# The gate modulation of layer 0 and all of layer 1's modulation from transposed weights, summed along the row

## The chip, the cores and the metric

The kernel runs on one core of a Trainium2 chip. The metric is the device time of one execution in microseconds (us), given as the median of several runs. The engines named below are PE (TensorE, the matmuls), PEld (TensorE's weight loads, which overlap its matmuls), DVE (VectorE), ACT (ScalarE), POOL (GpSimd) and SP (SyncE, which here issues nearly all transfers). Each engine runs its own list of instructions strictly in order; an instruction whose input is not ready holds everything behind it on that engine.

## The reference

Two layers work on 1024 latent and 256 context tokens of width 1024. Each layer first scales and shifts the normed tokens with numbers that come from a conditioning vector, and at its end multiplies the branch's output by a gate from the same source:

```python
def modulation(cond, w, b):                      # cond (1024,), w (1024, 3072)
    m = jax.nn.silu(cond) @ w + b
    return jnp.split(m, 3, axis=-1)              # shift, scale, gate
...
for i in range(DEPTH):                           # two layers
    sh_l, sc_l, g_l = modulation(c, mod_w[i], mod_b[i])
    sh_c, sc_c, g_c = modulation(c_ctx, mod_w[i], mod_b[i])
    h_lat = rms_norm(x_lat, norm_g[i]) * (1.0 + sc_l[:, None, :]) + sh_l[:, None, :]
    h_ctx = rms_norm(x_ctx, norm_g[i]) * (1.0 + sc_c) + sh_c
    ...                                          # even: two attentions; odd: convolution, neighbourhood attention
    x_lat = x_lat + g_l[:, None, :] * y_lat
    if update_ctx:                               # layer 0 only
        x_ctx = x_ctx + g_c * y_ctx
return rms_norm(x_lat, final_g)
```

The modulation is thus a product of a 1024 x 3072 matrix with two vectors ("conditions" 0 and 1), per layer. Layer 0 needs shift and scale (parts 0 and 1) before anything else, its gate (part 2) only after the attention. Layer 1 needs shift and scale when layer 0 is done, and its gate for condition 0 alone.

## The kernel before

All large matmuls are done as three products of a high and a low half (`mm3`, L320 to L322), so every operand is split: ACT casts the high half and POOL or DVE subtracts it (`split`, L298 and L301).

The program has these stages (times from the trace). To about 80 us, the first loads, layer 0's shift and scale, the norm and the inputs `h`. To about 160 us, the projections of the first of four attention units (`fill0(0)`, the flag `solo` being set). To about 640 us, attention units 2, 3, 0 and 1 in that order, each woven by `weave` with the projections of the next. From about 640 to 900 us, the last unit's attention, woven with layer 0's output projection (`out0_part`, weights `wr` from `ev_wo`). Then layer 1.

A scheduler writes each engine's list from priorities. `later(LATE)` puts work behind other work that is ready (`LATE` is 100), and `issue_after` makes an instruction wait for another one, its anchor, on the anchor's engine.

The modulation is computed in two ways. `mod_half` (L171 to L191) uses PE with the weights as the moving operand, in the first stage only. `mod_half_v` (L195 to L234) makes 512 columns of one part for one or two conditions. It loads blocks of 128 rows of `mod_w` (two together, 512 KB, while `solo`; else one, 256 KB), and DVE adds each, times the condition's value of that row, into an accumulator `macc` of 128 x 512 (L216 for the first, L221 for the others; outside `solo` a few go to ACT and POOL by the table `MODP`, L218 and L219). Then PE sums each accumulator over the partitions with four matmuls against a vector of ones (`trm`, L227; each shows as two in the trace's counts), and DVE adds the bias (L228). The result `modT[l]` holds 24 columns per condition, column `o` being outputs 128 o to 128 o + 127.

Of layer 0's shift and scale one half-part goes through `mod_half_v` (the event "v" of `PLAN`) and three through `mod_half` ("m"). Layer 0's gate and all of layer 1 (seven steps of two conditions, and the gate of layer 1 for one) are made by the generator `mod_steps`. `tick`, called at every third row block of a projection, advances it: at each call while `solo` (`TICK0` 1), at every third call later (`TICK1` 3). The last of its sums starts at 439.6 us.

The other names in this text: `QL` (L390) is the low half of queries, DVE's work, which PE's scores `st` wait for; `mp` (L580, L591) is the maximum over a row of scores `mx`, `nmt` (L379) what is made of it; `qs` (L301) is the split of projected queries and keys; `x` at L1012 is the residual plus gate times the output projection `po`; `Od`, `gt`, `QH` and `QL` on SP are transfers of the attention's operands and results; `pl`, `gl` and `wl` are low halves of weights or probabilities made by a subtraction on POOL or DVE.

Of the kernel before, what the change touches and what calls it, by code (L numbers as in the profile page):

```python
# [18 lines left out]
P = 128  # L19
# [32 lines left out]
MWB, WRB = 2, 2  # L52
# [21 lines left out]
TICK0, TICK1 = (1, 3)  # L74
# [15 lines left out]
def tile_kernel(ctx: ExitStack, tc: tile.TileContext, a, out):  # L90
# [11 lines left out]
    mk, mwp, hold, layer = [0], [None], [0], [0]  # L102
# [10 lines left out]
    def nm(s):  # L113
        uid[0] += 1
        return f"{s}_{uid[0]}"
# [79 lines left out]
    def mod_half_v(pool, l, part, j, conds):  # L195

        c0 = part * 1024 + j * 512
        pool, tag, bufs = (kvp, "QH", 3) if mwp[0] is not None else (pool, "macc", 2)
        accs = [pool.tile([P, 512], F32, tag=tag, name=nm("macc"), bufs=bufs) for _ in conds]
        pre = []  # L200
        for dk in range(DK):
            if solo[0] and dk % 2 == 0:
                w2 = mw_tile()
                d_ = SY.dma_start(w2, a["mod_w"][l, dk * P : (dk + 2) * P, c0 : c0 + 512].rearrange("(d p) n -> p d n", d=2))
                if mwp[0] is not None:
                    mm0.append(d_)
                pre = [w2[:, 0, :], w2[:, 1, :]]
            if pre:
                w = pre.pop(0)
                hold[0] = len(pre)  # L210
            else:
                w = pool.tile([P, 512], F32, tag="mw", name=nm("mw"), bufs=MWB)
                SY.dma_start(w, a["mod_w"][l, dk * P : (dk + 1) * P, c0 : c0 + 512])
            for q, t in zip(conds, accs):
                if dk == 0:
                    VE.tensor_scalar(t, w, csil[:, dk, q : q + 1], None, op0=ALU.mult)  # L216
                elif dk in MODP[q] and not solo[0]:
                    SC.activation(w, w, AF.Identity, scale=csil[:, dk, q : q + 1])  # L218
                    GP.tensor_tensor(t, t, w, op=ALU.add)  # L219
                else:  # L220
                    VE.scalar_tensor_tensor(t, w, csil[:, dk, q : q + 1], t, op0=ALU.mult, op1=ALU.add)  # L221
            yield
        o = part * 8 + j * 4
        for n_, (q, t) in enumerate(zip(conds, accs)):
            tr = bank("ov" if solo[0] else "tr", nm("trm"))
# [8 lines left out]
        yield  # L234
# [419 lines left out]
    with ExitStack() as p0x:  # L654
# [6 lines left out]
        with tc.tile_pool(name="st0", bufs=1, reuse_waits="tile") as st0:  # L661
# [38 lines left out]
            for ev in PLAN:  # L700
# [13 lines left out]
                elif ev == "v":  # L714
                    run(mod_half_v(st0, 0, *mh.pop(0), (0, 1)))
# [25 lines left out]
        def tick():  # L741
            beat[0] += 1
            if beat[0] % (TICK0 if solo[0] else TICK1) == 0:
                with later(LATE):
                    if mark[0] is None or solo[0]:
                        next(mods, None)
                    else:
                        with tc.issue_after(mark[0].ins):
                            next(mods, None)
# [128 lines left out]
        while hold[0]:  # L878
            next(mods)
# [96 lines left out]
    with tc.tile_pool(name="o0", bufs=1, reuse_waits="tile", side="right") as op_:  # L976
# [3 lines left out]
        x1 = []  # L980
        def load_oh(fs):
# [33 lines left out]
        def out0_part(fs):  # L1015
            for e2 in range(4):
# [58 lines left out]
        weave(main, NSTEP[U1 // 2] - GL - O1[0] - O1[1] - O1[2], through_attention(), O1[3])  # L1075
        a0x.close()
# [506 lines left out]
def _layout(i):  # L1583
    i = {n: np.asarray(i[n]) for n in _INS}

    def pk(v):
        return v.reshape(-1, P).T
# [5 lines left out]
    d["mod_w"] = i["mod_w"]  # L1593
# [49 lines left out]
```

## Time and profile before

| quantity | value |
|---|---|
| median of 3 runs | 1566.65 us (1564.84 to 1571.33) |
| span of the profiled execution | 1569.6 us |
| modulation weights loaded by SP | 34 transfers of 512 KB and 28 of 256 KB |
| the accumulations of L221 and L216 on DVE | 123, from 14.3 to 439.6 us |
| the sums of L227 on PE | 128 counted, from 33.5 to 442.0 us |

The profiled execution has no time beside its span; the span is the figure that stands next to the runs' times, 2.95 us above their median. In the profile a line of instructions reads: line, engine, operation, output from inputs with partitions x elements, the count, then busy time and the mean in ns of one, then the idle time ahead of them with what ended it. In a timeline a row reads start, duration, engine, line, operation, and in brackets the idle time ahead of it with what released it. A window row gives, for each engine, busy microseconds and the number of instructions in brackets, then the clock granted to PE as a share of full speed (PEclk), the share of time the transfer engines were busy, and the bytes moved.

### The profile page before, as it was taken

The page shows a single profiled execution, that of the slowest core. Times are in us where ns is not written, and L with a number is a line of the kernel's source. Part 1 is how long each engine was busy: PE and PEld are TensorE (multiplying, and loading weights), DVE is VectorE, ACT ScalarE, POOL GpSimd, SP SyncE. Part 2 cuts the span into 40 slices and gives each one's busy share as a digit, 9 for nine tenths or more (in the row PEclk, how much of TensorE's full clock was granted, in tenths as well). Part 3 has the DMA queues.
Part 4 walks back from the last instruction along what each step waited for, and adds up shares of the span by engine and source line. Part 5 has one row for each costly group of instructions (what it writes and reads, how often), then busy time and mean ns, then how long its engine had stood idle before and what let it go on. Part 6 is the DMA issues. An engine that isn't in the chain of part 4 may idle for free.

```text
span 1569.6 us, 22251 instructions
## 1 busy us (share of the span) xinstructions
PE 1460.8 (93%) x6984; PEld 1178.9 (75%) x6984; DVE 1129.4 (72%) x2172; ACT 762.0 (49%) x1545; POOL 830.0 (53%) x762
## 2 busy tenths in 40 slices
PE   6989999998999999899999889999999999899995
PEld 1878877876888677588887568888887787677784
DVE  4898896797768677455488668999654466776776
ACT  2721354545454754655555746443343445545472
POOL 1561463555465675756545756665443333444575
PEclk9899999999999999999999989999999999799897
DMA  9548245424431225612112022214547888889632
GB/s 337 190 142 260 87 142 167 132 67 125 154 116 47 67 91 167 224 47 61 48 38 85 14 94 61 81 58 148 177 154 224 237 229 242 248 231 251 187 95 108
DMA packets 199438, 221.03 MB, mean 141 GB/s; under 512 B 18956, under 2 KB 155352, under 8 KB 199320
## 3 DMA queue, kind: packets, MB, share of 16 engines
q1 hardware_dynamic: 192656, 208.04, 43.5%
q10 hardware_dynamic: 6664, 11.57, 2.3%
q8 instruction: 55, 0.90, 0.2%
q14 instruction: 63, 0.52, 0.1%
HBM read 159.51 MB, written 60.03 MB: 140 GB/s over the span
## 4 chain that ended last, share of the span: by engine, by line
PE 65%; DVE 14%; DMA 11%; issue 4%; POOL 2%; SPq 2%; ACT 1%; ACTq 0%; DVEq 0%; POOLq 0%
PE p L322 6%; PE p L321 6%; PE p L320 6%; PE ov L411 4%; PE ov L413 4%; PE ov L412 4%; PE po L320 4%; PE po L321 4%; PE po L322 4%; PE st L467 4%; PE st L471 4%; DMA mw<-in_mod_w_dram 3%; DVE macc L221 2%; PE pq L322 2%; PE pq L321 2%
## 5 line engine op out<-in xcount | busy, mean ns | idle before, releaser
L301 POOL TENSOR_TENSOR pl<-pf,ph 128x512 fp32r<-128x512 f32 (+4 forms) x321 | 393.7, 1237 | 320.1 <-ACT ph L298 260.0
L301 POOL TENSOR_TENSOR wl<-wr,wh 128x256 fp32r<-128x256 f32 (+2 forms) x256 | 197.5, 788 | 203.1 <-ACT wh L298 192.4
L479 ACT ACTIVATE pf<-st 128x512 f32<-128x512 f32 x284 | 167.3, 597 | 177.4 <-PE st L471 138.3
L298 ACT CAST ph<-pf 128x512 fp32r<-128x512 f32 (+4 forms) x364 | 210.5, 588 | 28.9 <-PE ov L412 21.5
L298 ACT CAST wh<-wr 128x256 fp32r<-128x256 f32 (+2 forms) x264 | 102.8, 404 | 172.9 <-DMA wr<-in_ev_qkv_dram 40.4
L320 PE MATMUL p<-hh,wh 128*128 128x512 f32 x448 | 177.5, 398 | 2.9 <-DVE spk L301 1.5
L321 PE MATMUL p<-hl,wh 128*128 128x512 f32 x448 | 178.0, 398 | 0.2 <-POOL hl L301 0.2
L322 PE MATMUL p<-hh,wl 128*128 128x512 f32 x448 | 175.9, 400 | 0.1
L467 PE MATMUL st<-QH,KAt 128*128 128x512 f32 (+4 forms) x364 | 145.4, 401 | 11.4 <-ACT pf L479 9.7
L411 PE MATMUL ov<-ph,Vt 128*128 128x512 f32 (+4 forms) x364 | 143.5, 394 | 9.7 <-ACT ph L298 5.0
L413 PE MATMUL ov<-pl,Vt 128*128 128x512 f32 (+4 forms) x364 | 144.1, 396 | 6.8 <-POOL pl L301 3.6
L471 PE MATMUL st<-QL,KBt 68*128 68x512 f32 (+4 forms) x364 | 139.0, 391 | 5.8 <-DVE QL L390 5.7
L412 PE MATMUL ov<-ph,Vt 128*64 128x512 f32 (+4 forms) x364 | 140.5, 386 | 0.0
L1122 DVE SCALAR_TENSOR_TENSOR cps<-U,taps,cps 128x512 f32<-128x512 f32 x184 | 124.3, 748 | 0.0
L591 DVE TENSOR_REDUCE mp<-mx 128x1 f32<-128x512 f32 x128 | 85.7, 682 | 42.5 <-PE mx L590 41.8
L221 DVE SCALAR_TENSOR_TENSOR macc<-mw,csil,macc 128x512 f32<-128x512 f32 x107 | 94.5, 901 | 17.5 <-DMA mw<-in_mod_w_dram 16.7
L320 PEld LDWEIGHTS p<-hh,wh 128*128 128x128 f32 x448 | 84.6, 189 | 23.6 <-DVE spk L301 1.7
L321 PEld LDWEIGHTS p<-hl,wh 128*128 128x128 f32 x448 | 84.5, 189 | 20.4 <-POOL hl L301 0.6
L322 PEld LDWEIGHTS p<-hh,wl 128*128 128x128 f32 x448 | 84.8, 189 | 20.1 <-POOL wl L301 0.6
L467 PEld LDWEIGHTS st<-QH,KAt 128*128 128x128 f32 x364 | 71.2, 196 | 33.4 <-ACT pf L479 17.6
L413 PEld LDWEIGHTS ov<-pl,Vt 128*128 128x128 f32 x364 | 71.1, 195 | 32.5 <-POOL pl L301 7.8
L411 PEld LDWEIGHTS ov<-ph,Vt 128*128 128x128 f32 x364 | 71.3, 196 | 27.3 <-ACT ph L298 8.4
(277 smaller groups left out, 3546.2 us busy)
## 6 DMA issues: line engine op xcount, KB each, us to landing
mw<-in_mod_w_dram SPq DMA_DIRECT2D x34, 512.0 KB, 5.9
Q<-qs SPq DMA_DIRECT2D x40, 256.0 KB, 2.7
QH<-Q SPq DMA_DIRECT2D x80, 128.0 KB, 2.8
wr<-in_od_d_dram SPq DMA_DIRECT2D x64, 128.0 KB, 2.7
mw<-in_mod_w_dram SPq DMA_DIRECT2D x28, 256.0 KB, 3.3
wr<-in_ev_qkv_dram SPq DMA_DIRECT2D x32, 192.0 KB, 3.6
KAt<-KD SPq DMA_DIRECT2D x16, 384.0 KB, 6.2
wr<-in_od_wo_dram SPq DMA_DIRECT2D x48, 128.0 KB, 3.2
```

Of the source, the lines that this page charges most:

```text
L221: VE.scalar_tensor_tensor(t, w, csil[:, dk, q : q + 1], t, op0=ALU.mult, op1=ALU.add)
L298: SC.copy(hi, src)
L301: (GP if leng == "g" else VE).tensor_tensor(lo, src, hi.bitcast(F32), op=ALU.subtract)
L320: PE.matmul(o, lh, rh, start=first, stop=False)
L321: PE.matmul(o, lh, rl, start=False, stop=False)
L322: done[0] = PE.matmul(o, ll, rh, start=False, stop=last)
L411: PE.matmul(o, V[:, 64:192], ph[:, :n], start=(t == 0), stop=False)
L412: PE.matmul(g.ov[0:64, q0 : q0 + n], V[:, 0:64], ph[:, :n], start=False, stop=False)
L413: pvs.append(PE.matmul(o, V[:, 64:192], pl[:, :n], start=False, stop=(last and g.sink is None)))
L467: sts.append(PE.matmul(st[:, :n], KA[:, cs], g.QH[:, q0 : q0 + n], start=True, stop=False))
L471: PE.matmul(st[:, :n], KB[0:68, cs], g.QL[0:68, q0 : q0 + n], start=False, stop=True)
L479: SC.activation(pf[:, :n], st[:, :n], AF.Exp, scale=1.0 if g.bias else SCALE)
```

## The change

`mod_half_v` is kept for the event "v" alone. Everything that `mod_steps` made is now made by `mod_rows` from `mod_wt`, a copy of the weights that the host gives transposed: one row is one output. A unit loads 128 rows of 1024 (512 KB, L241), and one DVE instruction (L251) multiplies them by `cb`, the condition's silu values laid out along the row and copied to all 128 partitions, sums along the row, and starts from the bias; the sum is one column of `modT`. In the order listing it shows as two rows, the product in place and the reading of the sum. There are 16 units for layer 0's gate (8 per condition), 24 for layer 1 condition 0 and 16 for condition 1: 56 in all. `cond_rows` makes the silu'd conditions as rows in DRAM (`csd`); `cb` is loaded from there four times in all, once for each condition of each layer.

The places and the buffers differ too. Layer 0's units use one buffer, and are advanced at every third beat, but no longer while `solo`. Layer 1's units use two buffers that an earlier stage has left free (`KB` and `KA` of the pool `a0`), and are advanced once after each block of layer 0's output projection, in the last attention unit. The anchor of `issue_after` is now `sts[-MLAG]`, a matmul of the scores.

The loads of modulation weights come to about 8.4 MB as blocks of `mod_w` and 56 x 0.524 = 29.4 MB as rows of `mod_wt`, against 34 x 0.524 + 28 x 0.262 = 25.2 MB before.

```diff
-MWB, WRB = 2, 2
+WRB = 2
-TICK0, TICK1 = (1, 3)
+TICK = 3
+MLAG = 2
...
-    def mod_half_v(pool, l, part, j, conds):
+    def mod_half_v(l, part, j, conds):
...
+    csd = dram("csd", [2, 1024])
+
+    def cond_rows(c_, t_):
+        SY.dma_start(c_[0:2, :], a["crow"])
+        SC.activation(t_[0:2, :], c_[0:2, :], AF.Tanh, scale=0.5)
+        VE.scalar_tensor_tensor(c_[0:2, :], t_[0:2, :], 1.0, c_[0:2, :], op0=ALU.add, op1=ALU.mult)
+        SY.dma_start(csd, c_[0:2, :])
+
+    def mod_rows(l, q, parts, cb, wt):
+        SY.dma_start(cb, csd[q : q + 1, :].broadcast_to([P, 1024]))
+        todo = [part * 8 + b for part in parts for b in range(8)]
+        ws = {}
+
+        def load(k):
+            o = todo[k]
+            ws[k] = wt()
+            r0 = (o - 16 if l == 0 else 8 + o) * P
+            SY.dma_start(ws[k], a["mod_wt"][r0 : r0 + P, :])
+
+        for k, o in enumerate(todo):
+            if l == 0:
+                load(k)
+                yield
+            else:
+                for k2 in range(k and k + 1, min(k + 2, len(todo))):
+                    load(k2)
+            w = ws.pop(k)
+            VE.tensor_tensor_reduce(out=w, in0=w, in1=cb, op0=ALU.mult, op1=ALU.add, scale=0.5,
+                                    scalar=modb[:, l, o : o + 1], accum_out=modT[l][:, o, q : q + 1])
+            if o == 15:
+                VE.scalar_tensor_tensor(gs[l][:, :, q], modT[l][:, 8:16, q], 1.0, normg[:, l, :], op0=ALU.add, op1=ALU.mult)
+            yield
...
         def tick():
             beat[0] += 1
-            if beat[0] % (TICK0 if solo[0] else TICK1) == 0:
-                with later(LATE):
-                    if mark[0] is None or solo[0]:
-                        next(mods, None)
-                    else:
-                        with tc.issue_after(mark[0].ins):
-                            next(mods, None)
+            if not solo[0] and beat[0] % TICK == 0:
+                with later(LATE), tc.issue_after(sts[-MLAG].ins if len(sts) >= MLAG else mark[0].ins):
+                    next(mods, None)
...
         def mod_steps():
-            for part in (2,):
-                for j in range(2):
-                    yield from mod_half_v(ap, 0, part, j, (0, 1))
-            for part in range(3):
-                for j in range(2):
-                    yield from mod_half_v(ap, 1, part, j, (0, 1) if part < 2 else (0,))
+            cb = ap.tile([P, 1024], F32, tag="cb", name="cb0")
+            wt = lambda: ap.tile([P, 1024], F32, tag="mw", name=nm("mw"))
+            cond_rows(cb, wt())
+            for q in range(2):
+                yield from mod_rows(0, q, (2,), cb, wt)
...
+        spare = [a0.tile([P, NTOK], F32, tag=t, name=nm("mw1"), bufs=2)[:, 0:1024] for t in ("KB", "KA")]
+        cb1 = a0.tile([P, 1920], F32, tag="V", name="cb1", bufs=2)[:, 0:1024]
+
+        def wt1():
+            spare.append(spare.pop(0))
+            return spare[-1]
+
+        mods1 = chain(mod_rows(1, 0, (1, 0, 2), cb1, wt1), mod_rows(1, 1, (1, 0), cb1, wt1))
...
                     for c in range(3):
                         yield from out0(fs, e, c, *w)
+                        with later(LATE), tc.issue_after(sts[-MLAG].ins):
+                            next(mods1, None)
...
         weave(main, NSTEP[U1 // 2] - GL - O1[0] - O1[1] - O1[2], through_attention(), O1[3])
+        run(mods1)
```

The first place is DVE in the first unit's projections, about 95 us into the run before. `macc` and `mw` are accumulators and weights of the modulation, `rt` and `pc` belong to the rotary step. Before:

```order
L830 TENSOR_TENSOR pc_750<-pc_750,k_cs 128x2x320
L221 SCALAR_TENSOR_TENSOR macc_588<-mw_637,csil,macc_588 128x512
L221 SCALAR_TENSOR_TENSOR macc_589<-mw_637,csil,macc_589 128x512
L301 TENSOR_TENSOR qs_842<-trk_838,qs_842 128x384
L221 SCALAR_TENSOR_TENSOR macc_588<-mw_637,csil,macc_588 128x512
```

In the same place now:

```order
L322 TENSOR_TENSOR qs_732<-trk_728,qs_732 128x384
L845 TENSOR_TENSOR rt_123_772<-pc_701,k_cs 128x320 x2
L847 TENSOR_TENSOR pc_701<-pc_701,k_cs 128x2x320
L322 TENSOR_TENSOR qs_767<-trk_763,qs_767 128x384
L845 TENSOR_TENSOR rt_132_852<-pc_781,k_cs 128x320 x2
L847 TENSOR_TENSOR pc_781<-pc_781,k_cs 128x2x320
```

The accumulations between the splits `qs` and the rotary steps are gone; nothing of the modulation stands there.

The second place is DVE while the second unit is projected (135 to 227 us before), where layer 0's gate is now made. `modT_90` is layer 0's result. Before, accumulations for both layers stood here:

```order
L221 SCALAR_TENSOR_TENSOR macc_1018<-mw_1108,csil,macc_1018 128x512 x2
L221 SCALAR_TENSOR_TENSOR macc_1018<-mw_1152,csil,macc_1018 128x512
L228 TENSOR_TENSOR modT_91<-trm_1176,modb 128x4
L221 SCALAR_TENSOR_TENSOR macc_1018<-mw_1152,csil,macc_1018 128x512
L216 TENSOR_SCALAR macc_1217<-mw_1219,csil 128x512
```

Now:

```order
L251 ISA mw_1560,modT_90<-mw_1560,cb_1139,modb 128x1024
L251 ISA modT_90 128x1
L406 TENSOR_TENSOR nmt_1332<-se_1334,nmt_1332 128x4
L601 TENSOR_REDUCE mp_1438<-mx_1440 128x2
L601 TENSOR_REDUCE mp_1438<-mx_1457 128x2
L251 ISA mw_1723,modT_90<-mw_1723,cb_1139,modb 128x1024
L251 ISA modT_90 128x1
L411 TENSOR_TENSOR QL_1117<-trn_1349,k_bd 12x512
```

Sums stand one by one ahead of `nmt`, `mp` and `QL`, each on the same buffer, whose next load follows the sum. The 16 sums of layer 0 stand within some 135 rows of DVE.

The third place is the last attention unit, on DVE and on SP, where layer 1 is now made. `mp` is the attention's, `x` the output projection's. DVE before, from about 790 us:

```order
L591 TENSOR_REDUCE mp_8269<-mx_8317 128x1
L1012 SCALAR_TENSOR_TENSOR x_1892_7482<-po_8764,modT_90,x_1892_7482 128x512
L591 TENSOR_REDUCE mp_8269<-mx_8320 128x1
L423 RECIPROCAL r_2126_8348<-r_2125_8347 128x8
L1012 SCALAR_TENSOR_TENSOR x_1901_7508<-po_8790,modT_90,x_1901_7508 128x512
```

DVE now:

```order
L251 ISA mw_1820_7188,modT_91<-mw_1820_7188,cb_7190,modb 128x1024
L251 ISA modT_91 128x1
L612 TENSOR_REDUCE mp_8055<-mx_8148 128x1
L612 TENSOR_REDUCE mp_8055<-mx_8151 128x1
L444 RECIPROCAL r_2071_8136<-r_2070_8135 128x8
L251 ISA mw_1821_7189,modT_91<-mw_1821_7189,cb_7190,modb 128x1024
L251 ISA modT_91 128x1
L1035 SCALAR_TENSOR_TENSOR x_1837_7231<-po_8719,modT_90,x_1837_7231 128x512
```

The sums stand between the same instructions as before. Layer 1's 40 sums (80 rows) stand within 200 rows of DVE, and PE's list has 504 rows beside these. On SP there, before:

```order
L331 DMA wr_8732<-in_ev_wo_dram 128x256
L331 DMA wr_8738<-in_ev_wo_dram 128x256
L331 DMA wr_8857<-in_ev_wo_dram 128x256
L331 DMA wr_8863<-in_ev_wo_dram 128x256
L565 DMA QH_7861<-Q_5_114 64x2x256 x2
L565 DMA QL_7862<-Q_5_114 64x2x256
```

SP now:

```order
L241 DMA mw_1820_7188<-in_mod_wt_dram 128x1024
L352 DMA wr_9052<-in_ev_wo_dram 128x256
L241 DMA mw_1821_7189<-in_mod_wt_dram 128x1024
L352 DMA wr_9058<-in_ev_wo_dram 128x256
L241 DMA mw_1820_7188<-in_mod_wt_dram 128x1024
L241 DMA mw_1821_7189<-in_mod_wt_dram 128x1024
L241 DMA mw_1820_7188<-in_mod_wt_dram 128x1024
L590 DMA gt_8242<-G_149 128x2x128
L241 DMA mw_1821_7189<-in_mod_wt_dram 128x1024
L352 DMA wr_9064<-in_ev_wo_dram 128x256
```

Each load of `mw` waits on SP until the sum before it on the same buffer is done, and what follows in SP's list (weights `wr`, gates `gt`) is issued after it.

More of the change, by code (lines that the diff above doesn't have):

```diff
@@ L101, in tile_kernel @@
     turn = [0, 0]
-    mk, mwp, hold, layer = [0], [None], [0], [0]
+    mk, mwp, layer = [0], [None], [0]
     sts, pvs = [], []
@@ L223, in mod_half_v @@
         o = part * 8 + j * 4
-        for n_, (q, t) in enumerate(zip(conds, accs)):
-            tr = bank("ov" if solo[0] else "tr", nm("trm"))
+        for q, t in zip(conds, accs):
+            tr = bank("ov", nm("trm"))
             for i in range(4):
@@ L1593, in _layout @@
     d["mod_w"] = i["mod_w"]
+    d["mod_wt"] = np.concatenate([i["mod_w"][0][:, 2048:].T, i["mod_w"][1].T])
+    d["crow"] = np.stack([i["c"][0], i["c_ctx"]])
     d["mod_b"] = np.stack([pk(i["mod_b"][l]) for l in range(2)], 1)
```

41 lines of the change are left out of this document (12 added, 29 removed).

## Prediction

> **What bounds the kernel now.** I read the page first (engines, the chain that ended last, the transfers), then a table of busy times by stretch, then the tiles of the modulation, then timelines at the places where PE waits.
>
> ```profile
> span 1569.6 us, 22251 instructions
> PE 1460.8 (93%) x6984; PEld 1178.9 (75%) x6984; DVE 1129.4 (72%) x2172; ACT 762.0 (49%) x1545; POOL 830.0 (53%) x762
> PE 65%; DVE 14%; DMA 11%; issue 4%; POOL 2%; SPq 2%; ACT 1%; ACTq 0%; DVEq 0%; POOLq 0%
> L221 DVE SCALAR_TENSOR_TENSOR macc<-mw,csil,macc 128x512 f32<-128x512 f32 x107 | 94.5, 901 | 17.5 <-DMA mw<-in_mod_w_dram 16.7
> mw<-in_mod_w_dram SPq DMA_DIRECT2D x34, 512.0 KB, 5.9
> mw<-in_mod_w_dram SPq DMA_DIRECT2D x28, 256.0 KB, 3.3
> ```
>
> PE is busy 93% of the span and holds 65% of the chain, so a microsecond taken from PE's own work counts nearly whole, and DVE time counts only where PE waits for it. Where that is, the table by stretch tells (busy microseconds, instructions in brackets):
>
> ```profile
> core 0: us, PE busy (x) PEld busy (x) DVE busy (x) ACT busy (x) POOL busy (x), PEclk, DMA share, GB/s
> 80.00:130.00 50.00, 42.27 (x245) 38.45 (x244) 47.31 (x61) 12.82 (x30) 28.16 (x19) 0.97 0.59 176
> 135.00:227.00 92.00, 87.79 (x472) 76.69 (x471) 81.35 (x160) 33.24 (x76) 39.71 (x33) 0.96 0.45 138
> 227.00:450.00 223.00, 209.80 (x1072) 174.95 (x1071) 175.50 (x388) 106.17 (x236) 114.47 (x97) 0.98 0.44 133
> 450.00:525.00 75.00, 73.97 (x364) 62.02 (x363) 53.67 (x99) 40.57 (x76) 48.07 (x38) 1.00 0.18 53
> 700.00:800.00 100.00, 100.00 (x482) 81.12 (x482) 59.39 (x111) 50.99 (x94) 56.31 (x49) 1.00 0.17 50
> ```
>
> From 80 to 130 (projections of the first unit) DVE is the bound: 47.31 of 50 busy, PE idle 7.7. From 227 to 450 (attention with layer 1's modulation in it) PE idles 13.2. From 450 to 525, the same kind of work with no modulation, it idles 1.0. From 700 to 800 (last unit, with layer 0's output projection) PE never idles, and DVE has 40.6 us free. The change takes modulation out of the first and third of these and puts it into the second and the last.
>
> **The change part by part.**
>
> *The `trm` products go (gain 10).* Sixteen groups of eight matmuls summed the accumulators over partitions; two groups stay (the "v" event), 14 go.
>
> ```profile
> L227 PE MATMUL trm<-one,macc x128: 165/251/272, 33.5 to 442.0; 128*128 128x2 f32 x128
> 189.27 0.95 PE L227 MATMUL trm<-one,macc 128*128 128x2 f32 x8
> ```
>
> A group takes 0.95 us of PE: 14 x 0.95 = 13.3. Some stand where PE idles anyway, so I take 10 (ends 7 and 13.3).
>
> *First unit's projections without modulation (gain 7).* PE waited there for splits that stood in DVE's queue behind accumulations:
>
> ```profile
> 98.16 0.55 PE L840 MATMUL trk<-ident,pc 128*128 128x128 f32 x3 [2.75 <-DVE qs L301]
> 104.62 1.05 PE L227 MATMUL trm<-one,macc 128*128 128x2 f32 x8 [1.85 <-DVE macc L221]
> 94.96 2.68 DVE L221 SCALAR_TENSOR_TENSOR macc<-mw,csil,macc 128x512 f32<-128x512 f32 x2
> 97.56 0.54 DVE L301 TENSOR_TENSOR qs<-trk,qs 128x384 fp32r<-128x384 f32 x1
> ```
>
> The split at 97.56 came after 2.68 us of accumulation, and PE waited 2.75 us for it. Of 7.7 idle, at the pace of the stretch without modulation (1.0 per 75) 0.7 would remain: gain 7, ends 3 (the rest late for loads) and 7.7.
>
> *Layer 1 out of 227 to 450 (gain 6).* PE's idle 13.2 would be 3.1 at that same pace: at most 10.1. The longest wait shows the mechanism, a split `QL` standing behind an accumulation that itself waited for its load:
>
> ```profile
> 385.88 0.73 PE L471 MATMUL st<-QL,KBt 68*128 68x512 f32 x2 [4.47 <-DVE QL L390]
> 370.47 0.75 DVE L221 SCALAR_TENSOR_TENSOR macc<-mw,csil,macc 128x512 f32<-128x512 f32 x1 [1.52 <-DMA mw<-in_mod_w_dram]
> 384.37 0.75 DVE L221 SCALAR_TENSOR_TENSOR macc<-mw,csil,macc 128x512 f32<-128x512 f32 x1 [0.93 <-DMA mw<-in_mod_w_dram]
> 385.15 0.68 DVE L390 TENSOR_TENSOR QL<-trn,k_bd 12x512 fp32r<-12x512 f32 x1
> ```
>
> Of the 4.47 only 0.93 + 0.75 is the accumulation's; unit starts stay. I take 6 (ends 2 and 10).
>
> *The price of a new sum.* No row-sum of 1024 elements is in the trace. The nearest is the same instruction pair at smaller widths (the mask maxima, L599), and above it a full POOL subtraction:
>
> ```profile
> L599 DVE CUSTOM_DVE_ANT_0 mx<-mx,k_bm 128x384 f32<-128x384 f32 x48 | 26.5, 563 | 7.7 <-PE mx L598 7.1
> L599 DVE CUSTOM_DVE_ANT_0 mx<-mx,k_bm 128x256 f32<-128x256 f32 x16 | 6.7, 424 | 0.1
> L599 DVE DVE_READ_ACCUMULATOR2_ANT mp<- 128x1 f32 x64 | 8.1, 127 | 0.3
> 86.84 1.74 POOL L301 TENSOR_TENSOR gl<-gr,gh 128x512 fp32r<-128x512 f32 x1
> 87.36 1.77 DVE L221 SCALAR_TENSOR_TENSOR macc<-mw,csil,macc 128x512 f32<-128x512 f32 x1
> L221 DVE SCALAR_TENSOR_TENSOR macc<-mw,csil,macc x107: 735/751/2017, 15.4 to 439.6; 128x512 f32<-128x512 f32 x107
> ```
>
> From 256 to 384 elements it grows by 139 ns, 1.086 per element: 563 + 640 x 1.086 = 1258 ns, and 127 for reading the accumulator, together 1.38 us (ends: 1.2 if the two overlap, 2.0 if it waits often). The last rows show why it may wait: an accumulation took 1.77 us instead of 0.75 (the median, in the tile's row of minimum, median and maximum) beside a POOL subtraction, and both ended within a microsecond. Over all 107 the mean is 901, 0.15 above that median. A sum 1.7 times as long (1.26 over 0.75), reading two tiles as the accumulation does, meets 1.7 times as much: 0.25 us. A sum costs DVE 1.63 us.
>
> [...]
>
> *The load and its chain.* A 512 KB transfer of modulation weights took 5.9 us in the median, many of them in the crowded start; half as much took 3.3. I take the middle, 4.6, and 0.4 for the issue (from the row below, its median).
>
> ```profile
> L204 SPq DMA_DIRECT2D mw<-in_mod_w_dram x22: 367/379/657, 6.5 to 154.6; - x22
> ```
>
> With a buffer that is refilled only after its sum, one round lasts 0.4 + 4.6 + 1.63 = 6.6 us.
>
> [...]
>
> *Layer 0's gate among the second unit's projections (loss 9).* One buffer, 16 sums: 16 x 6.6 = 106 us, where the stretch they stand in, 135 to 227, has 92. DVE runs strictly in order, so a sum whose load is late holds back `QL`, `mp` and `nmt` behind it, and PE behind these. 106 - 92 = 14, less the 4.2 that PE idles there now, gives 10; I take 9. Ends: -4 (all rounds hidden, old idle gone) and +16 (2.0 us sums). cb's loads and SP's extra rows wait on nothing longer than this chain.
>
> *Layer 1 in the last unit (loss 24).* The order bunches the 40 sums into 200 rows of DVE, beside 504 rows of PE; at PE's pace of 700 to 800 (482 per 100 us) these are 104 us. DVE's own work: 120 other rows x 0.535 (59.39/111) = 64, and 40 x 1.38 = 55, together 119, less 0.08 a row that neighbours overlap, shown here (796.61 + 0.74 ends after 797.27):
>
> ```profile
> 796.61 0.74 DVE L1012 SCALAR_TENSOR_TENSOR x<-po,modT,x 128x512 f32<-128x512 f32 x1
> 797.27 0.68 DVE L591 TENSOR_REDUCE mp<-mx 128x1 f32<-128x512 f32 x1
> ```
>
> which for the 80 new rows is 6: 113, nine more than PE's 104. Waits beside POOL (busy 56.31 of 100 there) add 40 x 0.25 = 10: 123. The loads set a second floor: two buffers, so 20 rounds of 6.6 = 132 us. The longer binds, so 132 - 104 = 28 if nothing hides it; some DVE rows stand ahead with slack, so I take 24. Ends: 0 and 45. Held back are `mp` (PE's next scores wait), `x` (frees PSUM for `po`) and `wl`. The wait of `issue_after` holds nothing: it binds instructions on the engine of its anchor, which is PE, and the units have only SP and DVE rows.
>
> *Nothing:* `cond_rows` (four small instructions ahead of the first sum, in idle ACT and DVE rows) and the "v" event, whose work is the same; if uncovered, under 5 us.
>
> Sum: -10 - 7 - 6 + 9 + 24 = +10. On the profiled 1569.6 that is 1579.6; the median shown, 1566.65, is 2.95 lower, so 1576.7, said as 1577.
>
> **Rivals.**
> (a) *DVE's idle time takes the sums.* For it: 40.6 us of DVE idle per 100, and PSUM double buffers. Against it: 113 against 104, in order. The loads land in 3.3, nothing contends: -10 - 7 - 10 + 0 + 5 = -22, 1545.
> (b) *A smaller bunch effect.* The last stretch costs 16 and layer 0 costs 5, with rounds of about 6: -10 - 7 - 6 + 5 + 16 = -2, 1565, which this kernel can't tell from no change (within 0.5%, 7.8 us).
> (c) *SP in single file.* Every reload waits on SP for a sum, with weights and Q loads behind it:
>
> ```profile
> wr<-in_ev_wo_dram SPq DMA_DIRECT2D x32, 128.0 KB, 2.3
> ```
>
> Where six reloads stand nearly together, three rounds, 20 us, pass before the next `wr` or `QH`. If that meets an out-projection with no weights left, PE loses those 20 on top of the 10, less what a 2.3 us transfer hides, about 16: 1593. It decides once a `wr` is issued later than its split's row is reached; against it speaks that weights are buffered several blocks ahead.
> (d) *It isn't spread.* Already in the forecast: the order shows 40 sums within about 104 us.
>
> **How the numbers follow.** Forecast (1569 to 1586) 0.36; (a) 0.28; (b) 0.20; (c) 0.16. Slower by over 0.5% takes most of the forecast and (c); the forecast's lower edge falls within 0.5% and the upper edge of (b) beyond, and I set the two off: 0.52. Faster by over 0.5%: 0.28. Same: 0.20. The range goes from 1546, at (a), to 1600, above (c) by the 45 end.
>
> **What the profile after would show.** Right: PE idle under 2 us in 80 to 130; none of L227 after the start; L251 near 1.26 + 0.13 us; DVE over 90% busy and PE idle 20 to 30 us in the stretch from about 690; waits for `mw` ahead of L251 totalling over 20 us. Wrong: `mw` landing in under 4 us and PE still 100% busy there (then (a)); SP's queue with `wr` issued late (then (c)); or an L251 above 2 us, which would make it slower than all of these.

## The result, and the profile after

The changed kernel takes 1578.51 us (median of ten runs, 1573.49 to 1582.08) against 1568.7 us for the kernel before in the same runs: a ratio of 1.006, with a 95% interval of 1.0042 to 1.0077. It is slower, by 9.8 us; 1577 was forecast. The profiled execution has a span of 1572.4 us, at the low end of the ten.

The head of its page, with the chain that ended last:

```profile
span 1572.4 us, 22029 instructions
PE 1447.9 (92%) x6872; PEld 1163.8 (74%) x6872; DVE 1120.8 (71%) x2162; ACT 763.3 (49%) x1541; POOL 839.1 (53%) x757
PE 64%; DMA 15%; DVE 13%; issue 3%; SPq 2%; POOL 2%; ACT 1%; ACTq 0%; DVEq 0%; POOLq 0%
```

PE has 13 us less to do than before, and DVE 9 us less in all, yet the program is longer. The same stretches as in the prediction, of the changed kernel:

```profile
80.00:130.00 50.00, 43.44 (x238) 38.77 (x237) 22.71 (x34) 15.59 (x35) 24.02 (x20) 0.93 0.50 158
135.00:227.00 92.00, 82.60 (x423) 72.64 (x421) 63.60 (x129) 33.47 (x74) 36.53 (x27) 0.96 0.54 164
227.00:450.00 223.00, 216.59 (x1113) 182.81 (x1114) 165.36 (x379) 114.34 (x253) 126.66 (x106) 1.00 0.39 118
700.00:800.00 100.00, 85.94 (x379) 65.15 (x377) 89.59 (x144) 40.41 (x75) 54.62 (x38) 0.97 0.68 198
```

PE's idle time from 227 to 450 has fallen from 13.2 to 6.4 us; from 135 to 227 it has risen from 4.2 to 9.4; from 700 to 800 from nothing to 14, beside a DVE that is 90% busy. The new sums, and the transfers that feed them:

```profile
L251 DVE CUSTOM_DVE_ANT_0 mw<-mw,cb,modb x56: 1234/1285/3345, 136.9 to 820.0; 128x1024 f32<-128x1024 f32 x56
L251 DVE DVE_READ_ACCUMULATOR2_ANT modT<- x56: 74/79/89, 138.1 to 821.3; 128x1 f32 x56
L251 DVE CUSTOM_DVE_ANT_0 mw<-mw,cb,modb 128x1024 f32<-128x1024 f32 x56 | 87.9, 1571 | 38.2 <-DMA mw<-in_mod_wt_dram 33.6 <-DMA cb<-csd 4.4
mw<-in_mod_wt_dram SPq DMA_DIRECT2D x56, 512.0 KB, 3.8
```

A sum takes 1.57 + 0.08 us in the mean, and DVE stood still 38 us ahead of them, nearly all for their loads.

To see where the 9.8 us arise, I set the two profiles side by side at equal work of PE: the time at which it had streamed as many columns, the products of L227 left out. At the point that the kernel before reaches at 160 us the changed one is 7 us ahead; at 227, 6; at 450, 19; at 690, 20. For the last unit I took the start of the 365th and the 505th of the 756 matmuls that write the scores: 698.7 and 875.4 us before, 678.5 and 884.6 after. The stretch between them grows from 176.7 to 206.1 us, so a lead of 20 turns into a lag of 9. Both kernels over just this stretch, before and then after:

```profile
698.70:875.40 176.70, 173.70 (x819) 137.83 (x817) 121.61 (x216) 95.31 (x175) 100.19 (x84) 1.00 0.17 54
```

```profile
678.50:884.60 206.10, 185.29 (x820) 140.84 (x818) 176.85 (x297) 96.07 (x175) 117.17 (x84) 0.97 0.51 153
```

Of the 29 us more, 18 are PE idle (3.0 to 20.8) and 12 are PE busier with the same matmuls; the lower granted clock (1.00 to 0.97) makes some 6 of these, and the others I can't place. From there to the end the changed profile is 6 us shorter (687.8 for 694.2), at a granted clock of 0.96 for 0.95, which I take for noise.

In some of the runs below, PE's list has up to 20 more instructions between these two scores, so that the stretch is not the same work there. For a comparison across runs I therefore take a longer one, from the same 365th score to the first product of layer 1's projections. It holds the same 1010 matmuls, as many of each kind, in every run that is compared by it. Before and then after, it grows by 29 us too:

```profile
698.70:929.40 230.70, 219.93 (x1011) 172.52 (x1010) 157.93 (x275) 130.88 (x247) 135.52 (x120) 0.96 0.17 51
678.50:938.50 260.00, 231.78 (x1012) 175.97 (x1011) 215.18 (x357) 131.36 (x247) 152.55 (x121) 0.94 0.43 132
```

What PE waited for between the two scores, in the changed kernel (total us, times, longest):

```profile
PE po L341 <- DVE x L1035: 11.7, 8, 2.8
PE mx L611 <- DVE mp L612: 3.3, 4, 1.3
PE mx L599 <- DMA QH<-Q: 2.1, 1, 2.1
```

These are `x` and `mp`, the rows that stand behind sums on DVE, and one transfer of queries. DVE in its turn waited there for the loads of the new sums:

```profile
DVE mw L251 <- DMA mw<-in_mod_wt_dram: 7.9, 9, 1.5
DVE mw L251 <- DMA cb<-csd: 2.7, 2, 2.1
```

### The profile page after: what moved, and what is told of

It is laid out like the page before. It is cut to its first block, busy times and chain, and to the rows that moved or that the text cites. A ratio compares the mean times of both kernels' runs of the same rounds, so it can differ in the third digit from the quotient of the medians.

```text
span 1572.4 us, 22029 instructions
## 1 busy us (share of the span) xinstructions
PE 1447.9 (92%) x6872; PEld 1163.8 (74%) x6872; DVE 1120.8 (71%) x2162; ACT 763.3 (49%) x1541; POOL 839.1 (53%) x757
## 4 chain that ended last, share of the span: by engine, by line
PE 64%; DMA 15%; DVE 13%; issue 3%; SPq 2%; POOL 2%; ACT 1%; ACTq 0%; DVEq 0%; POOLq 0%
PE p L343 6%; PE p L342 6%; PE p L341 6%; DMA mw<-in_mod_wt_dram 4%; PE ov L432 4%; PE ov L434 4%; PE ov L433 4%; PE st L488 3%; PE st L492 3%; DVE mw L251 3%; PE po L341 3%; PE po L342 3%; PE po L343 3%; DMA QH<-QD 2%; PE pq L343 2%
## 5 line engine op out<-in xcount | busy, mean ns | idle before, releaser
L322 POOL TENSOR_TENSOR pl<-pf,ph 128x512 fp32r<-128x512 f32 (+4 forms) x321 | 411.5, 1292 | 295.5 <-ACT ph L319 254.2
L251 DVE CUSTOM_DVE_ANT_0 mw<-mw,cb,modb 128x1024 f32<-128x1024 f32 x56 | 87.9, 1571 | 38.2 <-DMA mw<-in_mod_wt_dram 33.6
L488 PEld LDWEIGHTS st<-QH,KAt 128*128 128x128 f32 x364 | 70.5, 194 | 29.0 <-ACT pf L500 13.3
```

The source lines that it names most:

```text
L251: VE.tensor_tensor_reduce(out=w, in0=w, in1=cb, op0=ALU.mult, op1=ALU.add, scale=0.5, scalar=modb[:, l, o : o + 1], accum_out=modT[l][:, o ...
L322: (GP if leng == "g" else VE).tensor_tensor(lo, src, hi.bitcast(F32), op=ALU.subtract)
L488: sts.append(PE.matmul(st[:, :n], KA[:, cs], g.QH[:, q0 : q0 + n], start=True, stop=False))
```

## The experiments

Each ran beside the kernel before, whose median was 1568.9 us beside the runs without layer 1's units, with sums alone, with loads alone and with the units spread; 1569.1 beside those without layer 0's units, with one tile, with layer 1 earlier and with layer 0's gate the old way; 1569.7 beside those without the products of L227, with half sums and with layer 0's units earlier; and 1566.9 beside the last, with layer 1's gate later. The prices below are differences of medians, and the changed kernel's is 1578.5; as the kernel before shows, 3 us between two of them can be chance. The stretches and waits come from one profiled execution of each. The diffs are shortened.

### What each term is worth

**The last unit without layer 1's units.**

```diff
...
-                for k2 in range(k and k + 1, min(k + 2, len(todo))):
-                    load(k2)
...
-            VE.tensor_tensor_reduce(...)        # for layer 1 only
+            if k == 0 and q == 0:
+                GP.memset(modT[1], 0.25)
```

> Layer 1's 40 loads and 40 sums in the last unit are left out, and its modulation is filled with a constant. All theories: the whole price of the stretch goes. By the two traces the lead of the changed kernel over the one before turns there from 19.5 us to a lag of 11.5, so about 31 us: 1578.5 - 31 = 1547. If the price was my 24: 1554. If it stays above 1570, the loss was not made by these units at all.

Measured: 1545.22 us, ratio 0.9848 (0.9806 to 0.9891). The 40 units cost 33 us, and the longer stretch is back at 230.3:

```profile
679.70:910.00 230.30, 220.41 (x1012) 173.14 (x1011) 159.63 (x275) 130.76 (x247) 136.76 (x122) 0.96 0.17 53
```

So the whole loss of the change, and more, is made there.

**The second unit without layer 0's units.** The loads and sums of layer 0 are left out in the same way (`load(k)` and the sum for `l == 0`; `modT[0]` gets a constant).

> Layer 0's 16 loads and sums in the second unit are left out and its gate is filled with a constant. By my term (9 us lost, and the old idle of 4 gained): 1566 to 1570. By the waits of PE in the trace from 130 to 230 us that lead back to VectorE (some 12 us): 1567. If the chain is hidden: 1576 to 1580.

Measured: 1566.63 us, ratio 0.9989 (0.9969 to 1.0008): 12 us. At equal work of PE it leads the changed kernel by about 10 us at 227 us and again at 690. In the changed kernel's profile DVE's and PE's waits between 130 and 230 us show the mechanism:

```profile
DVE mw L251 <- DMA mw<-in_mod_wt_dram: 25.7, 11, 3.6
```

```profile
PE trn L410 <- DVE nmt L406: 5.4, 2, 4.1
```

The sums at the head of DVE's list wait 26 us for their loads, and what stands behind them makes PE wait.

**The kernel before without the products of L227.**

```diff
...
-                PE.matmul(tr[:, 2 * i : 2 * i + 2], t[:, i * P : (i + 1) * P], one, start=True, stop=True)
-            VE.tensor_tensor(modT[l][:, o : o + 4, q], tr[...], modb[:, l, o : o + 4], op=ALU.add)
+            VE.tensor_tensor(modT[l][:, o : o + 4, q], t[:, 0:4], modb[:, l, o : o + 4], op=ALU.add)
```

> The kernel before, without the 14 groups of sums over the partitions on PE (the bias is added to four columns of the accumulator instead, so the gate of layer 0 and layer 1's modulation are not the reference's). It measures the first term of my sum by itself. My 10 us: 1557 to 1560. If PE had room for them beside other waits: 1565 to 1570. If they also held other work back: under 1555.

Measured: 1563.25 us, ratio 0.9964 (0.9942 to 0.9987): 6 us, between 2 and 9. PE's own time, 13.3, was not wholly on the path. (The two groups of the "v" event stay.)

### What in a unit costs: the sum, the load, or the wait beside POOL

**Sums without reloads.**

```diff
+            w, wo = keep            # two tiles, loaded once
-            VE.tensor_tensor_reduce(out=w, in0=w, in1=cb, ...)
+            VE.tensor_tensor_reduce(out=wo, in0=w, in1=cb, ...)
```

> The 40 sums stay, but all read one tile loaded once (its product goes to the other spare buffer), so nothing is reloaded and no sum waits for a transfer; 38 loads are left out, and the results of layer 1's modulation are not the reference's. If VectorE's own time bounds the stretch: most of the loss stays, only the waits for loads go (10 us in the trace), 1569 to 1574. If the chain of load and sum bounds it: nearly all goes, 1547 to 1555.

Measured: 1586.97 us, ratio 1.0106 (1.0072 to 1.0139), slower than with the loads.

**Loads with sums of 8 columns.**

```diff
-            VE.tensor_tensor_reduce(out=w, in0=w, in1=cb, ...)
+            VE.tensor_tensor_reduce(out=w[:, :8], in0=w[:, :8], in1=cb[:, :8], ...)    # layer 1
```

> All loads stay, each sum of layer 1 takes 8 columns instead of 1024 (part of the computation is left out). If VectorE's own time bounds the stretch: nearly the whole loss goes, 1547 to 1553. If the chain of load and sum, or SP's single file, bounds it: a round is still 0.4 + 3.8 + 0.3 us for two units in place of about 6, some 10 to 15 us stay, 1558 to 1563 or more.

Measured: 1570.07 us, ratio 1.0006 (0.9985 to 1.0028). Both of my theories fail on the pair: by the medians the 40 units cost 42 us without their loads, 25 without their sums, and 33 with both. The two runs over the longer stretch, sums first, then loads, and what DVE waited for in the second:

```profile
685.20:943.30 258.10, 235.12 (x1011) 178.94 (x1010) 218.00 (x356) 130.26 (x246) 159.68 (x121) 0.93 0.18 55
```

```profile
683.10:940.50 257.40, 232.66 (x1012) 177.51 (x1011) 172.84 (x357) 130.24 (x247) 135.30 (x121) 0.93 0.43 133
```

```profile
DVE mw L252 <- DMA mw<-in_mod_wt_dram: 44.8, 26, 3.5
DVE mw L252 <- DMA cb<-csd: 3.3, 2, 3.0
```

Here lies the point. With sums alone DVE is busy 218.0 us and waits 1.3 for `cb`: its list is held 219 us. With loads alone it is busy 172.8 and stands 48.1 us at a tiny sum whose load is late: held 221. In the changed kernel it is busy 215.2 and waits 10.6: held 226. The three stretches are 258, 257 and 260 us, where the kernel without the units has 160 held and 230. So here a wait at the head of DVE's list held the rows behind it as work did, and taking away one of the two causes only let the other fill its place.

The medians lie further apart (42, 25 and 33 us) than these stretches (28, 27 and 30 us more than without units), and the stretch does not explain that. The profile with sums alone is 7 us behind the changed one already at the 365th score, where the lists of all engines are still the same, and loses 10 more behind the stretch. Of these 10 some 3 come from another order of PE's list in the program's final norm, where its products `bc` wait for the scale `nr`; first with sums alone, then in the changed kernel:

```profile
PE bc L289 <- DVE nr L269: 6.2, 2, 3.9
PE bc L284 <- DVE nr L264: 0.6, 1, 0.6
```

The last 23 matmuls and what follows them take 18.7 us instead of 15.8. The three other runs with this order are those with one tile, with layer 1's gate later and with layer 0's units earlier.

**Sums half as long, no reloads.** I formed that account from the runs above and tested it by halving the sums' columns (`[:, :512]`) where nothing waits for a load.

> As the run with sums and no reloads, but each of layer 1's sums takes 512 columns instead of 1024 (half of the product is left out). The account so far: what counts is the time for which VectorE's list is held, by work or by a sum at its head that waits for its load; that was 182 to 185 us of some 210 in the changed kernel, with sums alone and with loads alone, and 116 without the units. Here it would be about 116 + 40 x 0.75 = 146. If the price goes with the time held: half of the 40 us between 1587 and 1545, 1563 to 1569. If it needs a VectorE that is nearly full: 1548 to 1556. If it is a price per sum, whatever its length: 1580 or more.

Measured: 1557.81 us, ratio 0.9927 (0.9899 to 0.9956): 12.6 us above the kernel without units.

```profile
682.10:922.10 240.00, 222.63 (x1011) 172.27 (x1010) 201.94 (x356) 130.13 (x246) 143.23 (x121) 0.96 0.19 59
L257 DVE CUSTOM_DVE_ANT_0 mw<-mw,cb,modb 128x512 f32<-128x512 f32 x40 | 43.3, 1081 | 3.0 <-DMA cb<-csd 2.4
```

It came out between my two forecasts. The half sums took 1.08 us, not 0.75, so over the longer stretch DVE was held 204 us (2.4 of them waiting for `cb`), 45 more than without units, for 10 us more time (13 by the medians); in the other three runs 60 to 66 us more held gave 27 to 30. The price falls when DVE is held less, and not to nothing: a price per sum whatever its length is excluded.

**Sums that read one tile.**

```diff
-            VE.tensor_tensor_reduce(out=w, in0=w, in1=cb, ...)
+            VE.tensor_reduce(modT[l][:, o, q : q + 1], w, axis=AX.X, op=ALU.add)    # layer 1
```

> Each of layer 1's sums becomes a plain sum along the row of the loaded weights, which reads one tile instead of two (the product with the condition is left out); the size is the same. If the wait against GpSimd's instructions costs (1.57 us mean against 1.23 at the least, 40 times 0.3, and as much on GpSimd): 1578 falls by 10 to 15, to 1564 to 1568. If only VectorE's bare time counts: 1574 to 1580.

Measured: 1579.76 us, ratio 1.0069 (1.0047 to 1.0091): against the changed kernel no difference. Its sums, with what they waited for, and the longer stretch:

```profile
L255 DVE TENSOR_REDUCE modT<-mw 128x1 f32<-128x1024 f32 x40 | 48.5, 1213 | 18.5 <-DMA mw<-in_mod_wt_dram 18.3
682.70:934.80 252.10, 227.82 (x1012) 172.67 (x1011) 199.62 (x315) 130.33 (x246) 136.98 (x121) 0.96 0.45 135
```

Both engines' rows are shorter: a sum falls from 1571 to 1213 ns, and POOL's subtraction `pl` between the two scores, first after, then with one input, from 1516 to 1310 (before: 1301):

```profile
L322 POOL TENSOR_TENSOR pl<-pf,ph 128x512 fp32r<-128x512 f32 x63 | 94.8, 1516 | 64.2 <-ACT ph L319 51.4 <-PE st L492 6.9 <-PE po L343 4.3
```

```profile
L325 POOL TENSOR_TENSOR pl<-pf,ph 128x512 fp32r<-128x512 f32 x64 | 83.1, 1310 | 65.2 <-ACT ph L322 50.5 <-PE po L346 5.1 <-PE st L495 3.4
```

So POOL lost some 0.2 us a subtraction beside the sums of two tiles, and next to nothing beside those of one. The operation changed with the number of tiles (a plain sum for a product and a sum), and which of the two does it is not shown. A part of what the sums gave back, the loads took: the waits ahead of the sums grew from 10.6 to 18.3 us, and DVE was held 199.6 + 18.3 = 218 us, 8 less than in the changed kernel. The stretch is 8 us shorter too (252.1 for 260.0). That this does not show in the time is not the stretch's doing: the profile is 4 us behind at its start, where the lists are still the same, and loses 9 behind it, some 3 of them in the final norm as above. What the second tile and the product cost, nothing by the medians or up to 8 us by the stretch, this run does not settle.

### Where the units stand

**Spread along the last unit.** Each sum is held behind every second maximum of the attention, with the anchor on DVE.

```diff
...
+                while len(red) - n0 > 2 * k:
+                    with later(LATE), tc.issue_after(red[-1].ins):     # red: the maxima, L601 and L612
+                        next(mods1, None)
+                    k += 1
```

> Each sum of layer 1 is held behind every second maximum of the attention on VectorE itself, so that the 40 stand in 263 rows of VectorE instead of 188. If VectorE's own time bounds the stretch: its share falls from 98% to about 85%, and the loss from 31 to 10 or 15 us, 1557 to 1563. If each sum costs PE a wait wherever it stands: no change, 1574 to 1580. If the chain of loads bounds it: as good as without the units, 1547 to 1552.

Measured: 1585.11 us, ratio 1.0095 (1.0063 to 1.0127), slower than bunched. The stretch between the two scores, which holds the same matmuls here, is shorter, 197.8 us for the 206.1:

```profile
683.00:880.80 197.80, 181.34 (x819) 139.59 (x817) 164.62 (x276) 95.75 (x175) 115.14 (x84) 0.96 0.44 138
```

but the 9 sums that were left then fell into the change of layers, which needs them, and that piece (to layer 1's first projection) took 63.4 us instead of 53.9, at a granted clock of 0.75:

```profile
880.80:944.20 63.40, 53.37 (x194) 38.96 (x193) 49.38 (x82) 35.54 (x72) 41.31 (x36) 0.75 0.33 101
```

31 sums in the stretch for 21 us are 0.7 us each, as bunched (29 us for 40), and both pieces together, the longer stretch, take as long as in the changed kernel (260.0):

```profile
683.00:944.20 261.20, 234.70 (x1012) 178.55 (x1010) 214.01 (x357) 131.28 (x247) 156.45 (x119) 0.91 0.41 129
DVE mw L251 <- DMA mw<-in_mod_wt_dram: 4.1, 6, 1.6
```

**Layer 1's units earlier.** They follow layer 0's through its single buffer, one at every second beat, from about 230 to 485 us. Each load is now issued right behind the sum ahead of it, for layer 0 too, whose sums stand where they stood (139 to 227 us).

```diff
-TICK = 3
+TICK = 2
...
+            if k + 1 < len(todo):
+                load(k + 1)         # behind sum k, for both layers
...
             for q in range(2):
                 yield from mod_rows(0, q, (2,), cb, wt)
+            yield from mod_rows(1, 0, (1, 0, 2), cb, wt)
+            yield from mod_rows(1, 1, (1, 0), cb, wt)
```

> Layer 1's 40 units follow layer 0's through the same single buffer, one at every second beat of the projections, so that they lie from about 230 to 500 us, and none is in the last unit. If what costs is the bunch in the last unit: its 31 us go and some waits of the kernel before (13 us of PE idle from 227 to 450, of which 3 would be there anyway) come back, 1552 to 1560, faster than the kernel before and the changed one. If a sum costs wherever it stands on VectorE (busy 165 of 223 us there already): 1572 or more.

Measured: 1600.08 us, ratio 1.0203 (1.0169 to 1.0237). A clear miss for me: 55 us above the kernel without them, 1.4 us a sum. The stretch, then the same 1126 matmuls in the kernel without layer 1's units:

```profile
225.00:500.00 275.00, 242.34 (x1126) 198.66 (x1125) 225.71 (x468) 114.51 (x254) 143.68 (x108) 0.92 0.59 179
221.20:447.50 226.30, 220.12 (x1126) 187.17 (x1125) 167.52 (x381) 115.24 (x254) 130.53 (x109) 0.98 0.40 122
```

and the wait ahead of the sums in the first:

```profile
DVE mw L247 <- DMA mw<-in_mod_wt_dram: 26.2, 23, 4.0
```

The stretch is 49 us longer. DVE is held 252 us where it was held 169 (1.5 of them waiting for layer 0's last load), and about 18 of the 49 us are the granted clock, 0.92 for 0.98 (an estimate, 275 x 0.08 less 226.3 x 0.02).

**Layer 1's gate later.** Its 8 units are made after the convolution instead, and 32 stay.

```diff
-        mods1 = chain(mod_rows(1, 0, (1, 0, 2), cb1, wt1), ...)
+        mods1 = chain(mod_rows(1, 0, (1, 0), cb1, wt1), ...)
...
+            mods2 = mod_rows(1, 0, (2,), cbg, ...)      # advanced at every third step of d_proj(1)
```

> The changed kernel, but layer 1's gate (8 of the 40 units, needed only by the last output projection) is made after the convolution, about 1130 to 1200 us, where VectorE is busy 30 of 50 us and what stands behind on its list feeds transfers more than PE. The 32 others stay in the last unit, in 143 rows. If a sum's price depends on what stands behind it on VectorE's list, the 8 are free there and 32 instead of 40 cost less, by 0.8 us each or more: 1568 to 1573. If a sum costs the same 0.7 us wherever it stands: 1577 to 1580. If the bunch is as dense as before and its density is the price: 1575 or more, too.

Measured: 1577.63 us, ratio 1.0064 (1.004 to 1.0088), against the changed kernel no difference. The longer stretch fell from 260.0 to 248.2 us (32 sums, 18 us, or 0.6 each), a gain of 12. Behind it 8 us were lost again: layer 1's projections grew from 410.7 to 415.4, with 9.5 us of waits ahead of the 8 sums, and the final norm lost some 3 by its order as above. So the 8 sums were not free there either:

```profile
680.70:928.90 248.20, 226.11 (x1012) 173.99 (x1011) 204.46 (x341) 130.93 (x247) 148.57 (x119) 0.96 0.39 119
L251 DVE CUSTOM_DVE_ANT_0 mwg<-mwg,cbg,modb x8: 1276/1285/1793, 1138.2 to 1166.2; 128x1024 f32<-128x1024 f32 x8
```

**Layer 0's units earlier, and layer 0's gate the old way.** In the first, `tick` advances the units at every beat while `solo` too, and the anchor of `issue_after` is left out for all of them; in the second `mod_half_v` and its ticks are as in the kernel before for layer 0's gate, and only layer 1 is new.

```diff
-            if not solo[0] and beat[0] % TICK == 0:
-                with later(LATE), tc.issue_after(...):
+            if solo[0] or beat[0] % TICK == 0:
+                with later(LATE):
```

> The changed kernel with layer 0's 16 units advanced at every beat from the first unit's projections on, so that they stand some 60 rows earlier on VectorE, which was busy 23 of 50 us there. Left out altogether they gave 12 us. If sums are cheap where VectorE is half idle, though PE is not: 1570 to 1574. If a sum costs the same 0.7 us in both places: 1576 to 1580. If the loads collide there with the other transfers (the kernel moves 158 GB/s in that stretch): 1582 or more.

> Layer 0's gate is made as before (accumulations and sums on PE, in the first unit's projections), layer 1 as in the changed kernel. It tells what moving layer 0's gate is worth by itself. By my terms (4 us for four groups of sums on PE, 7 for the first unit's stretch, against a loss of 9): within 5 us of the changed kernel, 1580. By the traces, which show the changed kernel 3 us ahead at 285 us: 1581. If layer 0's chain in a single buffer costs more than the first unit's stretch gains: 1570 or less.

Measured: 1579.18 us (1.0059, 1.004 to 1.0078) and 1577.0 us (1.0063, 1.0038 to 1.0087). Layer 0's gate costs 12 us by rows in the second unit, 13 partly in the first (some 3 of them in the final norm), and 10 by accumulation in the first. Three ways, no difference that counts. With the first, DVE waited 43.4 us for loads between 80 and 200 us:

```profile
DVE mw L251 <- DMA mw<-in_mod_wt_dram: 43.4, 15, 4.6
```

No version here beats the kernel before: what was gained in one place was paid in another, by the medians at 0.7 to 1.0 us a sum (1.4 with layer 1 behind a single buffer).

## Why the prediction was right, and where it was not

The time (1577 for 1578.5), the sign and the place were right. By its steps:

- *The `trm` products, 10.* Measured 6, with 2 to 9 possible: too large. That more of them stood beside other waits than I allowed is likely, not shown.
- *First unit's projections, 7.* At 160 us the changed kernel leads by 7, and the kernel before without `trm` by 4, so about 3 are left for this term, its lower end. PE's idle time from 80 to 130 fell only from 7.7 to 6.6 us, where I expected under 2: instead of `qs` (5.2 us before) PE waited for a load of keys (2.7) and for another step of DVE (2.5). This term was too large.
- *Layer 1 out of 227 to 450, 6.* The lead grows from 6 to 19 there, by 14, of which `trm`'s share is at most 4 (four groups stand there). I took half of the idle time that the table allowed; the upper end, 10, was nearer. This term was mis-sized the other way, and with it the gain ahead of the last unit: 14 forecast, 20 measured.
- *Layer 0's gate, a loss of 9.* Measured about 10 at 227 us by progress, 12 by the medians, by the mechanism named: sums that wait for a single buffer's load at the head of DVE's list (25.7 us between 130 and 230).
- *The price of a sum, 1.63 us.* Measured 1.65 in the mean, 1.31 at the least.
- *Layer 1 in the last unit, a loss of 24.* Measured 29 by the profile and 33 by the medians, inside the ends of 0 and 45. But the step's reason was wrong: I set the chain of loads (132 us) against DVE's own time (113 to 123) and let the longer bind. The loads landed in 3.8 us and not in 4.6, which makes a round 5.9 us and 20 rounds 117, no more than DVE's time. The waits ahead of L251 there were 10.6 us, where I expected over 20; DVE's work was the larger part. The runs put the time held, work and waiting together, in place of the longer of the two. And the forecast has no term for the granted clock, which over the longer stretch took some 15 us where it took 9 before.
- Ahead of the last unit 6 us too little were gained, and in it 5 to 9 too little lost: these nearly cancel. That the total was better than its parts is luck.
- *Waits beside POOL.* I added 0.25 us a sum for them, 10 us in all; the mean of a sum, 1571 ns, was 0.34 us over the least, 1234. As a term of the time it stays open: the run with one tile left the median as it was and shortened the stretch by 8 us.
- *Rival (a)*, idle DVE takes the sums: it is refuted by 33 us. *Rival (b)*, a smaller bunch: refuted as to size. (The range's lower end, 1546, lies 1 us above the 1545 of the rival that it names.) *Rival (c)*, SP in single file: seen once, 2.1 us of PE waiting for `QH`; not 16.
- *The other signs.* DVE was 86% busy between the two scores and 90% from 700 to 800, not over 90; PE's idle time there, 21 us, and L251 at 1.29 + 0.08 us in the median came as said. `mw` landed in under 4 us, which I had called a sign for rival (a), but PE was not 100% busy.

The longer stretch says more than the medians. Each row gives, in us and from one profiled execution, how much longer DVE's list was held than without layer 1's units (159.6) and how much longer the stretch was (230.3):

| run | held longer | stretch longer | difference |
|---|---|---|---|
| half sums | 45 | 10 | 35 |
| layer 1's gate later, 32 units | 53 | 18 | 35 |
| sums that read one tile | 58 | 22 | 36 |
| sums without reloads | 60 | 28 | 32 |
| loads with sums of 8 columns | 61 | 27 | 34 |
| changed kernel | 66 | 30 | 36 |
| spread along the last unit | 58 | 31 | 27 |

About 35 us of held time cost nothing, and what came on top cost nearly its full length. Without the units DVE has 71 us in which its list is not held; with them 34 to 43 are left in each of these rows, and that part was never filled. Layer 1's units earlier fit as well (83 held longer, 49 us longer). I read this from the traces afterwards and made no run to test it. The spread units fit worst; their stretch lost some 24 us to the granted clock (0.91), the changed kernel's 15 (0.94), which may be why. Why just that part of DVE's idle time can't be used stays open.

## What to carry to other kernels

DVE, idle for a third of the longer stretch, was not free room there, as PE waits for short results in its list, which runs in order: 66 us of added work and waits in 71 us of idle time cost 30 us. Count a wait at the head of the list as work, expect that only a part of the idle time can be filled (here about half), and before you remove one of two causes (a load, a long instruction) check that the other does not fill its place. Compare stretches of two kernels only when they hold the same instructions of the bounding engine. And where two terms of an estimate are each unsure, a right total says little about them.

## What was not expected of the hardware

In the changed kernel a wait of PE of 2.12 us was followed, 2 us after its end, by a fall of the granted clock to 0.50. The wait, for a transfer:

```profile
745.40 0.59 PE L599 MATMUL mx<-KAt,QH 128*128 128x256 f32 x3 [2.12 <-DMA QH<-Q]
746.97 0.51 PE L341 MATMUL po<-hh,wh 128*128 128x512 f32 x1 [0.27 <-DVE x L1035]
```

and five of the windows of 1 us from there (the column ahead of the last two is the granted clock):

```profile
744.00:745.00 1.00, 0.00 (x0) 0.00 (x0) 0.71 (x1) 0.00 (x0) 1.00 (x1) 1.00 1.08 225
746.00:747.00 1.00, 0.73 (x6) 0.48 (x5) 1.00 (x4) 0.00 (x0) 0.00 (x0) 1.00 0.16 61
747.00:748.00 1.00, 1.00 (x3) 0.85 (x4) 1.00 (x1) 0.00 (x0) 0.00 (x0) 0.70 0.93 135
749.00:750.00 1.00, 1.00 (x4) 0.81 (x3) 0.00 (x0) 0.33 (x1) 0.00 (x0) 0.50 0.60 152
751.00:752.00 1.00, 1.00 (x6) 0.81 (x5) 0.95 (x4) 0.31 (x1) 1.00 (x1) 1.00 0.62 250
```

The idle time lies from 743.3 to 745.4; the clock falls to 0.50 at 747.4, when PE is busy again, and stays there for 3.4 us (an estimate from the means of the windows: 0.70 from 747, 0.50 twice, 0.60 from 750). Products of 128x512 that take 0.40 us from 751.2 take 0.63 in it (747.66 to 750.22), so if the wait brought the fall on, it cost up to 1.7 us more, half of the 3.4, beside its own 2.1. PE was busy for 1.7 of the 4.1 us from 743.3 to the fall. The wait of 2.79 us for `x` that ended at 785.02 stands beside such a fall too: the windows of 1 us from 784 to 788 show 0.97, 0.50, 0.50, 0.50 and 0.82, some 3.4 us again. That the waits bring the falls on is my reading of these two places, not shown by a run. Over the longer stretch one minus the clock, times its length, makes some 9 us before (0.96), 15 in the changed kernel (0.94) and 18 each in the runs with loads and with sums alone (0.93).
